# Value products of an attention stage: float32 matmuls on two halves of the array's columns in place of fp32r matmuls on high and low parts

## The chip, the cores and the metric

The kernel runs on one core of one Trainium2 chip. The metric is the device time of one execution in microseconds, the median of several runs. A profile, taken by the hardware profiler, shows one execution in detail. Engine names in it: PE is TensorE's matmuls and PEld its weight loads, DVE is VectorE, ACT is ScalarE, POOL is GpSimd, SP is SyncE, whose queue issues nearly all DMAs here.

## The reference

A trunk of two layers runs over 512 tokens and 16 learned meta tokens ahead of them (528 in all), 1024 wide, all in float32. In each layer one input projection gives the inputs of two mixers, a pooling mixer and a latent attention with 8 heads, and their gated sum goes through an output projection. Cut to what the change touches, the attention is:

```
kv = (c_kv @ w_kv_b).reshape(B, L, N_HEADS, QK_NOPE_DIM + V_HEAD_DIM)   # 64 + 64
k_nope, v = kv[..., :QK_NOPE_DIM], kv[..., QK_NOPE_DIM:]
...                                                                     # norms, rotary
s = einsum('bqhd,bkhd->bhqk', q, k) * scale      # causal, in blocks of 128 queries
p = softmax(where(valid, s, MASK_VALUE))
o = einsum('bhqk,bkhd->bqhd', p, v)
y_mla = (o.reshape(B, L, MLA_WIDTH) * silu(z_mla)) @ W_mla_up
```

Everything is float32, so the kernel has to keep float32's accuracy in its matmuls.

## The kernel before

**Numbers in two parts.** A matmul on fp32r operands keeps fewer bits than float32. The kernel therefore writes an operand as hi + lo, both fp32r: ScalarE copies the value into an fp32r tile (hi), VectorE subtracts hi from the value (lo). `mm3` (L204 to L208) makes a product from three matmuls, hi·hi, hi·lo and lo·hi. Nearly all of PE's work is of this kind: the rows of L205, L206 and L207. A few small sums (norms, L426, L501, L535, L707) are plain float32 matmuls with 16 or 32 columns of weights, placed with `tile_position=(0, 32 * g)` on four quarters of the array's columns.

**The main stream.** A generator, `stream`, walks a list of projections (`Gemm`s) in order. `step` issues its next few matmuls, `fill`, `fill_now` and `gap` issue as many as a given time would hold by a count in the code, and `after` hangs a step of the attention on that count. The projections so fill PE's time between the attention's matmuls. The framework's scheduler gives each engine its final order by readiness and the order of the code; `follow` ties two instructions of one engine in order without a wait, and `behind` makes an instruction wait for another, often the newest matmul of the stream.

**Attention, head by head.** `v_body` (L682) makes the values at the end of the projection v: for each of four blocks of 128 keys the result in PSUM is scaled and written to `vt`, 128 columns a head, 64 of hi (L700, ScalarE) and 64 of lo (L701, VectorE). `head` (L815) issues the scores of four blocks of 128 queries, their exponentials (`expo`) and 32x32 transposes on VectorE (`turn`) into the tile `attD`, which has ten blocks of 128 columns: the causal pairs of query block and key block. A DMA writes `attD` to DRAM (L906), and 7800 ns of the count later `back` (L912) issues four DMAs that read it back turned over into a tile `attE` (L915), keys on partitions. `parts` (L948) splits that tile, in two halves, into hi (L958, ScalarE, into a tile `th`) and lo (L959, VectorE, in place). `pv` (L962) makes the value products for the four key blocks j: key block j meets query blocks j to 3, so its matmul is 512, 384, 256 or 128 wide. For each j there are two matmuls into one PSUM tile `o`: at L980 all 128 columns of `vt` (hi and lo of the values) against hi of the probabilities, and at L983 the 64 columns of hi against lo. Rows 0 to 63 of `o` then hold hi·hi and hi·lo, rows 64 to 127 lo·hi. At L988 ScalarE copies one half of the rows, at L989 VectorE adds the other. The products of a head are issued while the scores of a later head are on their way: in `head`, `parts(prev)` comes first, then two gaps of main stream with the other work of the head, then `pv(late)`.

Of the kernel before, what the change touches and what calls it, by code (L numbers as in the profile page):

```python
# [9 lines left out]
F32 = mybir.dt.float32  # L10
F32R = mybir.dt.float32r
BF16 = mybir.dt.bfloat16
I32 = mybir.dt.int32
AF = mybir.ActivationFunctionType
ALU = mybir.AluOpType
# [3 lines left out]
P = 128  # L19
DEPTH = 2  # L20
D = 1024
# [3 lines left out]
HALF = T // 2  # L25
W = 528
WU = 544
H = 8
# [33 lines left out]
NB = 10  # L62
# [18 lines left out]
def trunk(ctx, tc, xT, xrow, mrow, pos, win, wkr, wqb, wkb, wvb, wgr, wpu, wmu, wout, gains, const, yT):  # L81
    nc = tc.nc
    pe, act, dve, gp, sp = nc.tensor, nc.scalar, nc.vector, nc.gpsimd, nc.sync

    cp = ctx.enter_context(tc.tile_pool(name="cp", bufs=1))
    sl = ctx.enter_context(tc.tile_pool(name="sl", bufs=1))
# [8 lines left out]
    def nm(s):  # L95
        uid[0] += 1
        return f"{s}_{uid[0]}"
# [5 lines left out]
        return tp.tile([P, w], F32, tag="tmp", name=nm("tmp"), bufs=3)  # L103

    def att(tag):
        return sl.tile([P, NB * P], F32 if tag == "D" else F32R, tag=f"att{tag}", name=nm(f"att{tag}"), bufs=1 if tag == "D" else 2)

    def wide():
        return tp.tile([P, NB * P], F32R, tag="th", name=nm("th"), bufs=2)

    def halves():
        for k in range(4, 8):
            for a, b in FULL:
                yield xb[:, k, a:b]
        for tag in "DE":
            t = att(tag)
            for a in range(4):
                yield t[:, HALF * a:HALF * a + HALF].bitcast(F32)

    def mmt():  # L120
        return pp.tile([P, 512], F32, tag="mm", name=nm("mm"), bufs=4)
# [56 lines left out]
    for j in range(2):  # L178
        gp.memset(qhl[0][j][96:128, :].bitcast(F32), 0.0)
        gp.memset(qhl[1][j][32:64, :].bitcast(F32), 0.0)  # L180
    vt = cp.tile([P, 4, H, P], F32R, name="vt")

    class Gemm:
        def __init__(self, name, src, width, evac=None, xs=None, segs=None, body=None):
# [25 lines left out]
    newest = [None]  # L210
# [95 lines left out]
    def follow(ins, other):  # L306
        tc.add_manual_dep(ins.ins, other.ins.name,
                          mybir.DependencyInfo(mybir.DependencyClass.NoSync, mybir.DependencyReason.SCHED_ONLY))

    def behind(ins, other):  # L310
        tc.add_manual_dep(ins.ins, other.ins.name,
                          mybir.DependencyInfo(mybir.DependencyClass.Sync, mybir.DependencyReason.DATA))
# [35 lines left out]
    class Layer:  # L348
# [333 lines left out]
        def v_body(self, k, w):  # L682
            self.vw.append(w)
            if k == 0:
                return
            wv, cs = self.vw, self.cs
            mc = sm.tile([P, 4 * NM], F32, tag="mc", name=nm("mc"))
            for k in range(2):
                h, l = (t[:, 0:NM].bitcast(F32).unsqueeze(1).to_broadcast([P, 2, NM]) for t in cs[k])
                dve.tensor_add(mc[:, 32 * k:32 * k + 32].rearrange("p (a b) -> p a b", a=2), h, l)  # L690
            self.vb = sm.tile([96, 512], F32R, tag="vb", name=nm("vb"))
            for j in range(4):
                ps = mmt()
                for k in range(2):
                    ch, cl = (t[:, NM + P * j:NM + P * (j + 1)] for t in cs[k])
                    mm3(ps, ch, cl, wv[k][0], wv[k][1], k == 0, k == 1)
                ci = self.ninv[:, j:j + 1]
                hi, lo = vt[:, j, :, 0:64], vt[:, j, :, 64:128]
                pv = ps.rearrange("p (a b) -> p a b", a=H)
                act.activation(hi, pv, AF.Copy, scale=ci)  # L700
                dve.scalar_tensor_tensor(out=lo, in0=pv, scalar=ci, in1=hi.bitcast(F32),  # L701
                                         op0=ALU.mult, op1=ALU.subtract)
                yield 6 * 216
            ps = mmt()
            for g in range(4):
                k, e = g % 2, 256 * (g // 2)
                mm = pe.matmul(ps[32 * g:32 * g + 32, 0:256], mc[:, 32 * k:32 * k + 32],  # L707
                               self.vgemm.raw[:, 512 * k + e:512 * k + e + 256], start=True, stop=True,
                               tile_position=(0, 32 * g))
                behind(mm, newest[0])  # L710
            vf, t = tmp(), tmp()
            for i in range(2):
                e = 256 * i
                act.activation(t[0:32, e:e + 256], ps[64 * i + 32:64 * i + 64, 0:256], AF.Copy)
                dve.tensor_add(t[0:32, e:e + 256], ps[64 * i:64 * i + 32, 0:256], t[0:32, e:e + 256])
            for e in range(2):
                v4 = [x[0:32, :512].rearrange("p (a e b) -> p a e b", a=4, e=2)[:, :, e, :] for x in (vf, t)]
                dve.tensor_scalar(v4[0], v4[1], self.ninv[0:32, 4:5], cst[0:32, C_VBD + e:C_VBD + e + 1],
                                  op0=ALU.mult, op1=ALU.mult)
            act.activation(self.vb[0:32, :], vf[0:32, :512], AF.Copy)  # L720
            dve.tensor_sub(self.vb[64:96, :], vf[0:32, :512], self.vb[0:32, :].bitcast(F32))
            act.activation(self.vb[32:64, :], vf[0:32, :512], AF.Copy)
            yield 6 * 216
# [91 lines left out]
        def head(self, h, kq, prev):  # L815
            kh, kl, qh, ql = kq
            odd = h % 2
# [85 lines left out]
            got = []  # L903
            n = NB * 32
# [7 lines left out]
            def back():  # L912
                got.append(att("E"))
                for b in range(4):
                    behind(sp.dma_start(got[0][32 * b:32 * b + 32, :].bitcast(F32).rearrange("k (a x) -> k a x", a=4),  # L915
                                        via[:, n * b:n * b + n].rearrange("(a k) x -> k a x", a=4)), newest[0])
                if odd == 0:
                    self.rb = slot("cq11")
                rb = self.rb
                behind(sp.dma_start(rb[64 * odd:64 * odd + 64, 0:512], row.partition_broadcast(64)), newest[0])  # L920
# [27 lines left out]
        def parts(self, prev):  # L948
            if prev is None:
                return None  # L950
            h, got = prev
            while not got:
                step()
            got = got[0]
            hi, f = wide(), got.bitcast(F32)
            for a in (0, NB * 64):
                b = a + NB * 64
                behind(act.activation(hi[:, a:b], f[:, a:b], AF.Copy), newest[0])  # L958
                dve.tensor_sub(got[:, a:b], f[:, a:b], hi[:, a:b].bitcast(F32))  # L959
            return h, hi, got  # L960

        def pv(self, prev, hosts=()):  # L962
            if prev is None:
                return
            h = prev[0]
            p, odd = h // 2, h % 2
            o = sct() if h == H - 1 else pp.tile([P, 512], F32, tag="o", name=nm("o"), bufs=1)
            hosts, last = list(hosts), [None]

            def chain(ins):  # L970
                if last[0] is not None:
                    follow(ins, last[0])
                last[0] = ins
                return ins

            for j in range(4):
                k0, n = block(j, j), 4 - j
                st = block(j + 1, j) - k0 if n > 1 else 1
                hi, lo = (t.rearrange("p (a s r) -> p s a r", a=4, s=NB)[:, k0:k0 + st * (n - 1) + 1:st] for t in prev[1:])
                chain(pe.matmul(o[:, P * j:512], vt[:, j, h, :], hi, start=j == 0, stop=j == 3))  # L980
                for fn in hosts[2 * j:2 * j + 2]:
                    chain(fn())
                chain(pe.matmul(o[0:64, P * j:512], vt[:, j, h, 0:64], lo, start=False, stop=j == 3, skip_group_check=True))  # L983
            if odd == 0:
                self.op = tmp()
            n0, m0 = (64, 0) if odd else (0, 64)
            op = self.op[n0:n0 + 64, NM:T]
            act.activation(op, o[m0:m0 + 64, :], AF.Copy)  # L988
            dve.tensor_add(op, o[n0:n0 + 64, :], op)  # L989
            if odd == 1:  # L990
                op, mt = self.op[:, NM:T], self.mt

                def part2():
                    m = mmt()
                    pe.matmul(m, self.vb[:, P * p:P * (p + 1)], mt[0:96, 0:512].rearrange("p (a i r) -> p i a r", a=4, i=4),  # L995
                              start=True, stop=True)
                    self.ogs[p] = (slot(f"q{p}", F32R), slot(f"kn{p}", F32R))
                    dve.tensor_add(op, m, op)
                    dve.tensor_mul(op, op, self.zms[p][:, NM:T])
                    split(*self.ogs[p], op, NM, T)  # L1000

                after((3 if p == 3 else 2) * LAG, part2)
# [293 lines left out]
```

## Time and profile before

| | |
|---|---|
| median of 3 runs | 756.11 us (755.23 to 756.22) |
| the profiled execution | 756.64 us, its span 754.9 us |
| PE busy | 749.7 us, 99% of the span |
| VectorE busy | 548.1 us |
| ScalarE busy | 395.9 us |
| HBM | 140 GB/s over the span |

The time of an execution is measured around the program; the span runs from its first to its last instruction in the profile. An instruction's duration on PE contains the depth of the pipeline, so matmuls that follow each other overlap in their rows, and what a matmul costs is read from its start to the start of the next. The attention of the first layer lies at about 163 to 312 us, that of the second at about 545 to 683 us. In rows such as `128*64 128x512` the first pair is rows and columns of the weights in the array, the second partitions and columns of the moving operand.

### The profile page before, as it was taken

To read this page: it belongs to the slowest core of one execution; us is meant where nothing else is said; L and a number is where in the kernel's file an instruction comes from. 1 tells how busy PE (TensorE), PEld (TensorE's weight loads), DVE (VectorE), ACT (ScalarE), POOL (GpSimd) and SP (SyncE) were. 2 spreads that over 40 slices of the span, in tenths; PEclk is the share of its full clock that TensorE was granted. 3 is DMA by queue.
4 is the path that set the end of the run, shared out by engine and by line. 5 is a ranking of instruction groups with operands and counts; after the bars stand their busy time and mean duration, and the time that the engine had idled before them with its cause. 6 is when DMAs were issued, how large, how long until landed. Compare 5 with 4: busy or idle time off the path is not lost.

```text
span 754.9 us, 14329 instructions
## 1 busy us (share of the span) xinstructions
PE 749.7 (99%) x5038; PEld 682.9 (90%) x5038; DVE 548.1 (73%) x1209; ACT 395.9 (52%) x866; POOL 218.8 (29%) x267
## 2 busy tenths in 40 slices
PE   9999999999999999999999999999999999999998
PEld 8999899999999999999997898887788888888887
DVE  5588777457999988684466477676478999975942
ACT  6755655645565665542355446456345666653321
POOL 1126404204463620061130264023044435111400
PEclk9999999999999999999999999999999999999999
DMA  8532223443765567525642322234447756773472
GB/s 316 162 108 89 74 82 86 113 116 119 211 186 166 151 194 192 156 86 157 183 145 85 114 84 66 89 90 120 108 135 210 190 156 181 195 200 93 127 227 84
DMA packets 72853, 106.58 MB, mean 141 GB/s; under 512 B 14102, under 2 KB 34966, under 8 KB 72780
## 3 DMA queue, kind: packets, MB, share of 16 engines
q1 hardware_dynamic: 72636, 105.39, 47.6%
q8 instruction: 40, 0.66, 0.4%
q14 instruction: 33, 0.27, 0.1%
q10 hardware_dynamic: 144, 0.26, 0.1%
HBM read 89.76 MB, written 15.86 MB: 140 GB/s over the span
## 4 chain that ended last, share of the span: by engine, by line
PE 98%; DMA 1%; ACT 0%; SPq 0%; issue 0%; DVE 0%; ACTq 0%
PE mm L205 29%; PE mm L207 29%; PE mm L206 29%; PE S L205 2%; PE S L207 2%; PE S L206 2%; PE o L980 1%; PE o L983 1%; PE S L535 1%; PE S L881 1%; DMA attE<-pdr 1%; PE S L501 0%; DMA xb<-xT 0%; PE mm L995 0%; PE mm L426 0%
## 5 line engine op out<-in xcount | busy, mean ns | idle before, releaser
L205 PE MATMUL mm<-hh,whi 128*128 128x264 f32 (+2 forms) x1072 | 336.1, 315 | 0.6 <-ACT whi L200 0.6
L206 PE MATMUL mm<-hl,whi 128*128 128x264 f32 (+2 forms) x1072 | 336.6, 315 | 0.0
L207 PE MATMUL mm<-hh,wlo 128*128 128x264 f32 (+2 forms) x1072 | 336.4, 316 | 0.0
L201 DVE TENSOR_TENSOR wlo<-raw,whi 128x512 fp32r<-128x512 f32 (+2 forms) x238 | 173.4, 730 | 95.8 <-ACT whi L200 92.4
L200 ACT ACTIVATE whi<-raw 128x512 fp32r<-128x512 f32 (+2 forms) x238 | 142.3, 600 | 176.1 <-PE mm L206 136.4
L205 PEld LDWEIGHTS mm<-hh,whi 128*128 128x128 f32 x1072 | 201.3, 188 | 15.0 <-issue 0.8
L206 PEld LDWEIGHTS mm<-hl,whi 128*128 128x128 f32 x1072 | 201.6, 188 | 12.9
L207 PEld LDWEIGHTS mm<-hh,wlo 128*128 128x128 f32 x1072 | 200.9, 188 | 12.3
L649 POOL TENSOR_TENSOR racc<-racc,tmp 128x264 f32<-128x264 f32 (+1 forms) x15 | 14.4, 959 | 132.3 <-ACT tmp L648 132.3
L1055 POOL TENSOR_TENSOR tmp<-tmp,xb 128x264 f32<-128x264 f32 (+1 forms) x24 | 27.0, 1137 | 49.1 <-DVE tmp L1053 46.4
L833 DVE CUSTOM_DVE_ANT_0 S<-S,maskw,nqs 128x240 f32<-128x240 f32 (+4 forms) x80 | 37.8, 492 | 4.2 <-PE S L207 3.9
L811 POOL CAST qhl<-q 32x528 fp32r<-32x528 f32 (+1 forms) x32 | 25.1, 800 | 44.2 <-PE S L881 42.9
L809 POOL CAST kh<-cq 32x528 fp32r<-32x528 f32 x16 | 15.6, 976 | 69.8 <-issue 36.1
L206 PE MATMUL mm<-th,whi 128*128 128x264 f32 (+1 forms) x108 | 34.7, 321 | 0.0
L205 PE MATMUL mm<-cq,whi 128*128 128x264 f32 (+1 forms) x108 | 34.7, 321 | 0.0
L205 PE MATMUL mm<-u,whi 128*128 128x264 f32 (+1 forms) x108 | 34.6, 321 | 0.0
L206 PE MATMUL mm<-cq,whi 128*128 128x264 f32 (+1 forms) x108 | 34.5, 321 | 0.0
L207 PE MATMUL mm<-cq,wlo 128*128 128x264 f32 (+1 forms) x108 | 34.5, 321 | 0.0
L207 PE MATMUL mm<-u,wlo 128*128 128x264 f32 (+1 forms) x108 | 34.5, 319 | 0.0
L959 DVE TENSOR_TENSOR attE<-attE,th 128x640 fp32r<-128x640 f32 x32 | 26.9, 862 | 3.7 <-ACT th L958 3.7
L840 ACT ACTIVATE cq<-S,bia 128x400 f32<-128x400 f32 (+2 forms) x48 | 24.4, 511 | 9.2 <-DVE bia L894 7.7
L843 POOL COPY pm<-cq 128x16 f32<-128x16 f32 x32 | 18.2, 570 | 37.7 <-ACT cq L840 37.5
(301 smaller groups left out, 1369.5 us busy)
## 6 DMA issues: line engine op xcount, KB each, us to landing
raw<-win SPq DMA_DIRECT2D x143, 256.0 KB, 3.2
pdr<-attD SPq DMA_DIRECT2D x16, 640.0 KB, 3.7
attE<-pdr SPq DMA_DIRECT2D x64, 160.0 KB, 3.9
raw<-wout SPq DMA_DIRECT2D x32, 256.0 KB, 2.8
raw<-wpu SPq DMA_DIRECT2D x16, 256.0 KB, 2.7
raw<-wmu SPq DMA_DIRECT2D x16, 256.0 KB, 2.7
raw<-wqb SPq DMA_DIRECT2D x12, 256.0 KB, 2.6
xb<-xT SPq DMA_DIRECT2D x8, 264.0 KB, 5.5
```

The lines of the kernel that those rows point to most:

```text
L200: act.activation(hi[:, :n], raw[:, :n], AF.Copy)
L201: dve.tensor_sub(lo[:, :n], raw[:, :n], hi[:, :n].bitcast(F32))
L205: first = pe.matmul(out, wh, xh, start=start, stop=False)
L206: pe.matmul(out, wh, xl, start=False, stop=False)
L207: newest[0] = pe.matmul(out, wl, xh, start=False, stop=stop)
L809: gp.tensor_copy(d[r0:r0 + 32, :], f[g0:g0 + 32, :])
L811: gp.tensor_copy(d[r0:r0 + 32, x0:T], f[g0:g0 + 32, x0:T])
L833: return dve.tensor_tensor_reduce(out=sv, in0=sv, in1=mask, scale=nqs[:, i, h:h + 1], scalar=3e38, op0=ALU.add, op1=ALU.min, accum_out=bia ...
L840: act.activation(pv, sv, AF.Exp, scale=-1.0, bias=bia[:, i:i + 1], accum_out=rs[:, c:c + 1])
L843: gp.tensor_copy(pm[:, i, 16 * odd:16 * odd + 16], pt[i][:, 0:NM])
L959: dve.tensor_sub(got[:, a:b], f[:, a:b], hi[:, a:b].bitcast(F32))
L1055: gp.tensor_add(t[:, :b - a], t[:, :b - a], self.am[m][:, a:b])
```

## The change

The probabilities and the values are no longer split. `vt` is a float32 tile with 64 columns a head, written by ScalarE alone. `attE` is float32, and `parts` only waits in the code until its loads have been issued. `pv` has one float32 matmul for each key block, with 64 columns of weights: blocks 0 and 3 go to one half of the array's columns and of `o`'s rows, blocks 1 and 2 to the other half, and each half sums its two blocks. ScalarE's copy and VectorE's add put the halves together; the first 128 queries meet key block 0 alone, so the add leaves them out.

```
 def att(tag):
-    return sl.tile([P, NB * P], F32 if tag == "D" else F32R, ...)
+    return sl.tile([P, NB * P], F32, ...)
...
-vt = cp.tile([P, 4, H, P], F32R, name="vt")
+vt = cp.tile([P, 4, H, 64], F32, name="vt")
...                                                # v_body
-    hi, lo = vt[:, j, :, 0:64], vt[:, j, :, 64:128]
-    pv = ps.rearrange("p (a b) -> p a b", a=H)
-    act.activation(hi, pv, AF.Copy, scale=ci)
-    dve.scalar_tensor_tensor(out=lo, in0=pv, scalar=ci, in1=hi.bitcast(F32),
-                             op0=ALU.mult, op1=ALU.subtract)
+    act.activation(vt[:, j], ps.rearrange("p (a b) -> p a b", a=H), AF.Copy, scale=ci)
...                                                # parts
-    got = got[0]
-    hi, f = wide(), got.bitcast(F32)
-    for a in (0, NB * 64):
-        b = a + NB * 64
-        behind(act.activation(hi[:, a:b], f[:, a:b], AF.Copy), newest[0])
-        dve.tensor_sub(got[:, a:b], f[:, a:b], hi[:, a:b].bitcast(F32))
-    return h, hi, got
+    return h, got[0]
...                                                # pv
-    for j in range(4):
+    n0, m0 = (64, 0) if odd else (0, 64)
+    for j in (0, 1, 2, 3):
         k0, n = block(j, j), 4 - j
         st = block(j + 1, j) - k0 if n > 1 else 1
-        hi, lo = (t.rearrange("p (a s r) -> p s a r", a=4, s=NB)[...] for t in prev[1:])
-        chain(pe.matmul(o[:, P * j:512], vt[:, j, h, :], hi, start=j == 0, stop=j == 3))
-        for fn in hosts[2 * j:2 * j + 2]:
-            chain(fn())
-        chain(pe.matmul(o[0:64, P * j:512], vt[:, j, h, 0:64], lo, start=False, stop=j == 3, ...))
+        x = prev[1].rearrange("p (a s r) -> p s a r", a=4, s=NB)[...]
+        c = m0 if j in (0, 3) else n0
+        mm = pe.matmul(o[c:c + 64, P * j:512], vt[:, j, h, :], x, start=j < 2, stop=j > 1, tile_position=(0, c))
+        if j:
+            follow(mm, last)
+        last = mm
...
     act.activation(op, o[m0:m0 + 64, :], AF.Copy)
-    dve.tensor_add(op, o[n0:n0 + 64, :], op)
+    dve.tensor_add(op[:, P:512], o[n0:n0 + 64, P:512], op[:, P:512])
```

More of the change, by code (lines that the diff above doesn't have):

```diff
@@ L105, in att @@
     def att(tag):
-        return sl.tile([P, NB * P], F32 if tag == "D" else F32R, tag=f"att{tag}", name=nm(f"att{tag}"), bufs=1 if tag == "D" else 2)
+        return sl.tile([P, NB * P], F32, tag=f"att{tag}", name=nm(f"att{tag}"), bufs=1 if tag == "D" else 2)
     def wide():
@@ L117, in halves @@
             for a in range(4):
-                yield t[:, HALF * a:HALF * a + HALF].bitcast(F32)
+                yield t[:, HALF * a:HALF * a + HALF]
     def mmt():
@@ L914, in back @@
                 for b in range(4):
-                    behind(sp.dma_start(got[0][32 * b:32 * b + 32, :].bitcast(F32).rearrange("k (a x) -> k a x", a=4),
+                    behind(sp.dma_start(got[0][32 * b:32 * b + 32, :].rearrange("k (a x) -> k a x", a=4),
                                         via[:, n * b:n * b + n].rearrange("(a k) x -> k a x", a=4)), newest[0])
@@ L953, in parts, with pv @@
                 step()
-            got = got[0]
-            hi, f = wide(), got.bitcast(F32)
-            for a in (0, NB * 64):
-                b = a + NB * 64
-                behind(act.activation(hi[:, a:b], f[:, a:b], AF.Copy), newest[0])
-                dve.tensor_sub(got[:, a:b], f[:, a:b], hi[:, a:b].bitcast(F32))
-            return h, hi, got
-        def pv(self, prev, hosts=()):
+            return h, got[0]
+        def pv(self, prev):
             if prev is None:
@@ L967, in pv @@
             o = sct() if h == H - 1 else pp.tile([P, 512], F32, tag="o", name=nm("o"), bufs=1)
[L968 to L974, printed above, removed]
-            for j in range(4):
+            n0, m0 = (64, 0) if odd else (0, 64)
+            for j in (0, 1, 2, 3):
                 k0, n = block(j, j), 4 - j
                 st = block(j + 1, j) - k0 if n > 1 else 1
-                hi, lo = (t.rearrange("p (a s r) -> p s a r", a=4, s=NB)[:, k0:k0 + st * (n - 1) + 1:st] for t in prev[1:])
-                chain(pe.matmul(o[:, P * j:512], vt[:, j, h, :], hi, start=j == 0, stop=j == 3))
-                for fn in hosts[2 * j:2 * j + 2]:
-                    chain(fn())
-                chain(pe.matmul(o[0:64, P * j:512], vt[:, j, h, 0:64], lo, start=False, stop=j == 3, skip_group_check=True))
+                x = prev[1].rearrange("p (a s r) -> p s a r", a=4, s=NB)[:, k0:k0 + st * (n - 1) + 1:st]
+                c = m0 if j in (0, 3) else n0
[3 more added lines that the diff above has]
+                last = mm
             if odd == 0:
                 self.op = tmp()
-            n0, m0 = (64, 0) if odd else (0, 64)
             op = self.op[n0:n0 + 64, NM:T]
             act.activation(op, o[m0:m0 + 64, :], AF.Copy)
-            dve.tensor_add(op, o[n0:n0 + 64, :], op)
+            dve.tensor_add(op[:, P:512], o[n0:n0 + 64, P:512], op[:, P:512])
             if odd == 1:
```

## The prediction

> **What bounds the kernel now.** First the first parts of the profile's page: the span, the busy times, the granted clock, the chain that ended last.
>
> ```profile
> span 754.9 us, 14329 instructions
> PE 749.7 (99%) x5038; PEld 682.9 (90%) x5038; DVE 548.1 (73%) x1209; ACT 395.9 (52%) x866; POOL 218.8 (29%) x267
> PEclk9999999999999999999999999999999999999999
> PE 98%; DMA 1%; ACT 0%; SPq 0%; issue 0%; DVE 0%; ACTq 0%
> ```
>
> The clock is full in all 40 slices, and 98% of the chain is PE. The change works in the two attention stages, so I cut the span there (busy time by stretch):
>
> ```profile
> 163.00:312.00 149.00, 148.95 (x1206) 147.42 (x1205) 126.47 (x331) 87.18 (x216) 53.77 (x72) 1.00 0.62 176
> 545.00:683.00 138.00, 138.00 (x670) 115.39 (x669) 119.92 (x275) 80.39 (x185) 48.50 (x72) 1.00 0.65 181
> ```
>
> The first column after the length is PE: 148.95 of 149.00 us and 138.00 of 138.00. The projections of the main stream fill every hole there, so PE never runs dry. VectorE is at 126.47 of 149.00 and 119.92 of 138.00, high but off the path. Only PE time counts: the question is how many us of array time the value products take before and after.
>
> **The value products now.** Sixteen heads with eight matmuls each, in these groups (by line: least, median and greatest duration, first and last start):
>
> ```profile
> L980 PE MATMUL o<-th,vt x56: 223/310/502, 210.1 to 673.1; 128*128 128x512 f32 x14, 128*128 128x384 f32 x14, 128*128 128x256 f32 x14, 128*128 128x128 f32 x14
> L980 PE MATMUL S<-th,vt x8: 223/313/403, 305.9 to 679.7; 128*128 128x512 f32 x2, 128*128 128x384 f32 x2, 128*128 128x256 f32 x2, 128*128 128x128 f32 x2
> L983 PE MATMUL o<-attE,vt x56: 220/312/404, 212.4 to 673.2; 128*64 128x512 f32 x14, 128*64 128x384 f32 x14, 128*64 128x256 f32 x14, 128*64 128x128 f32 x14
> L983 PE MATMUL S<-attE,vt x8: 221/311/403, 307.3 to 679.8; 128*64 128x512 f32 x2, 128*64 128x384 f32 x2, 128*64 128x256 f32 x2, 128*64 128x128 f32 x2
> ```
>
> Durations contain the pipeline's depth, so I count from start to start. A head whose eight stand together, and one that comes behind small matmuls (PE in order of time):
>
> ```profile
> 671.85 0.40 PE L206 MATMUL mm<-hl,whi 128*128 128x512 f32 x1
> 672.08 0.40 PE L980 MATMUL o<-th,vt 128*128 128x512 f32 x1
> 672.32 0.40 PE L983 MATMUL o<-attE,vt 128*64 128x512 f32 x1
> ...
> 673.20 0.23 PE L983 MATMUL o<-attE,vt 128*64 128x128 f32 x1
> 673.27 0.44 PE L207 MATMUL mm<-hh,wlo 128*128 128x512 f32 x1
> 673.55 0.39 PE L205 MATMUL mm<-hh,whi 128*128 128x512 f32 x1
> ```
>
> ```profile
> 221.53 0.17 PE L881 MATMUL S<-kh,qhl 128*16 128x16 f32 x1
> 221.56 0.48 PE L980 MATMUL o<-th,vt 128*128 128x512 f32 x1
> ...
> 222.84 0.33 PE L205 MATMUL mm<-hh,whi 128*128 128x264 f32 x1
> 223.02 0.28 PE L206 MATMUL mm<-hl,whi 128*128 128x264 f32 x1
> ```
>
> An ordinary 128x512 step is 0.23 to 0.24 us (671.85 to 672.08, 672.08 to 672.32), or 0.46 ns a column, and here the half-wide pass over low parts costs as much as the full one. The first head: 672.08 to 673.27 is 1.19, and the next step (673.27 to 673.55) is 0.28, 0.05 over its like: 1.24 us. The second: 221.56 to 222.84 is 1.28, plus 0.18 less 0.12 (a 128x264 step, below) behind it: 1.34. The same sum over the 128 rows of the four groups gives 1.23 to 1.56 us a head, 20.7 us together, 1.29 in the mean.
>
> **What takes their place.** Per head four float32 matmuls with 64 columns of weights: blocks 0 (512 wide) and 3 (128) on one half of the array's columns, blocks 1 (384) and 2 (256) on the other. No float32 matmul 64 columns wide is in the trace, but there are float32 matmuls on quarters of the columns, at L426, L501, L535 and L707. They give both prices. The pass:
>
> ```profile
> 405.21 0.41 PE L426 MATMUL mm<-cq,ones 128*32 128x264 f32 x1
> 405.22 0.41 PE L426 MATMUL mm<-q,ones 128*32 128x264 f32 x1
> 405.22 0.41 PE L426 MATMUL mm<-cq,ones 128*32 128x264 f32 x1
> 405.23 0.41 PE L426 MATMUL mm<-q,ones 128*32 128x264 f32 x1
> 405.46 0.39 PE L426 MATMUL mm<-cq,ones 128*32 128x264 f32 x1
> ...
> 406.12 1.96 PE L501 MATMUL S<-xb,kn 128*32 128x264 f32 x32
> 408.02 0.50 PE L205 MATMUL mm<-hh,whi 128*128 128x512 f32 x1
> 408.36 0.40 PE L206 MATMUL mm<-hl,whi 128*128 128x512 f32 x1
> ```
>
> L501 is written 16 times a layer and stands here x32: a float32 matmul is two passes. Four passes start within 0.02 us on the four quarters, the next four follow when these are through. The 32 are eight rounds of four: 1.96 less the last one's own 0.39 is 1.57 us for seven rounds, 0.224 us for 264 columns, or 0.85 ns a column, 1.85 times the 0.46 above. So a float32 matmul costs two passes of nearly double price each, but quarters run side by side at no visible loss. If halves do the same, block 0 and block 3 take 640 x 2 x 0.85 = 1.09 us, blocks 1 and 2 the same 640 columns, 1.09, beside it. The order 0, 1, 2, 3 fits: when block 0 ends (0.87), block 2's second pass starts and block 3 takes its half.
>
> That alone would be 0.2 us less than 1.29. But entering and leaving such a burst costs:
>
> ```profile
> 85.70 0.40 PE L207 MATMUL mm<-whi,kl 128*128 128x512 f32 x1
> 86.03 0.64 PE L707 MATMUL mm<-attD,mc 128*32 128x256 f32 x8
> 86.59 0.39 PE L205 MATMUL mm<-hh,whi 128*128 128x264 f32 x1
> 86.82 0.28 PE L206 MATMUL mm<-hl,whi 128*128 128x264 f32 x1
> 86.94 0.28 PE L207 MATMUL mm<-hh,wlo 128*128 128x264 f32 x1
> ```
>
> From 85.70 to 86.82 is 1.12 us. The two ordinary steps in it are 0.23 (512 wide) and 0.12 (264 wide, 86.82 to 86.94), which leaves 0.77 for the burst. Its eight passes are two rounds of 256 columns, 2 x 256 x 0.85 = 0.44. So 0.33 us are fixed: about 0.10 ahead, where the array's last full matmul must be through before the first weights go in, 0.23 behind, where the first full weights wait in the same way. The burst of the fence before leaves as slowly: its last passes are through at about 407.92 (406.12 + 1.57 + 0.224), and the second ordinary matmul comes at 408.36 instead of 408.15 (407.92 + 0.23), 0.21 later. The next rows add a little, since the first weights of a half take longer to load than those of a quarter:
>
> ```profile
> L983 PEld LDWEIGHTS o<-attE,vt x56: 133/135/139, 212.3 to 673.1; 128*64 128x64 f32 x56
> L707 PEld LDWEIGHTS mm<-attD,mc x16: 106/108/110, 86.0 to 465.5; 128*32 128x32 f32 x16
> ```
>
> That is 0.03 us once a burst. A head then takes 1.09 + 0.33 + 0.03 = 1.45 us, against 1.29: 0.16 x 16 = 2.5 us more.
>
> The Trainium skill, "TensorEngine Tiling (Array Packing)", section Key Properties, says that a change of tiling mode, not just of the tile, drains the array; it gives no price. The trace agrees, with the 0.33 us above. The page "TensorE: Matmul & The Clock Gate" of the Trainium skill, Part 3, speaks against the overlap itself: matmuls start and end strictly in program order. Here four starts stand within 0.02 us ahead of any fifth, and if the two passes of a matmul lie side by side in the queue, as one instruction's parts would, the second pass of the first was overtaken by the first passes of the other quarters. No row shows the queue's order, so this becomes a rival below.
>
> **What else goes or moves.**
>
> ```profile
> L958 ACT ACTIVATE th<-attE x32: 721/724/741, 206.4 to 674.9; 128x640 fp32r<-128x640 f32 x32
> L959 DVE TENSOR_TENSOR attE<-attE,th x32: 761/810/2182, 207.5 to 675.8; 128x640 fp32r<-128x640 f32 x32
> ```
>
> Off ScalarE go 32 copies, 32 x 0.72 = 23 us; off VectorE 32 subtracts, 32 x 0.81 = 26 us by the median, and the subtracts of L701, and a quarter of each add at L989. Worth to the end: nothing, because PE in these stages idles 0.05 us in 287. It could cost only if the freed engines let something else collide; every load keeps its issue (SP's queue is unchanged, 64 loads of attE), so I see nothing. The value tile shrinks by half, which nobody waits for.
>
> A wait moves: the products now wait on the four loads of attE themselves, on PE, where the copy on ScalarE stood between. Behind a waiting product stands the whole main stream. The chain of waits passes through the loads of attE at one head alone, the seventh of the first layer (start, length; below it PE in order of time):
>
> ```profile
> 285.25 4.36 DMA attE<-pdr
> ...
> 291.13 0.50 PE o L980
> ```
>
> ```profile
> 290.80 0.28 PE L205 MATMUL mm<-hh,whi 128*128 128x264 f32 x1
> ```
>
> The load lands at 289.61, the copies follow, and PE starts at 291.13, 0.33 behind a matmul whose step is 0.12: it stands idle for 0.2 us. Without the copies the product can come up to 1.5 us earlier; the cost of that wait lies between 0 (a load that is in when PE comes) and 1.5 us (a product queued just as early as the copies' absence allows, and a load that is late by as much). I take 0.2, as now, nearest to the row, so the difference is nil. In the other direction the readiness of all four products at one moment is a help: today the first head's low parts start at 212.4 and its high parts at 210.1 (first starts of the two groups), with projections between; from now on nothing should split the four.
>
> **Sum.** 16 x (1.45 - 1.29) = +2.5 us. The profiled run of before took 756.64 us with a span of 754.9; the median is 756.11, so the profiled one lies 0.5 above it. The forecast for the median is 756.1 + 2.5 = 758.6 (0.33%). What a measurement of this kernel can tell from no change is about 0.2%, 1.5 us.
>
> **The rivals.**
>
> *Passes start strictly in order.* Block 1's first pass then cannot start before block 0's second, at 0.435: block 1 ends at 1.09, block 2 at 1.52, and block 3 inside that. 1.52 + 0.36 = 1.88 a head, +0.59 x 16 = +9.4: 765.5 us. Against it: the four starts within 0.02 us. For it: they are on quarters, and the queue's order isn't shown. Chance 0.07.
>
> *Halves do not overlap at all.* 2 x 1.09 + 0.36 = 2.54 a head, +1.25 x 16 = +20: 776 us. Only if two 64-wide halves share something that four quarters do not; no row hints at it. 0.04.
>
> *The four are split by main-stream matmuls*, as the pairs are today. Block 0 alone (0.87), then the rest (1.09), and 0.36 twice: 2.68, +1.39 a head; in half of the heads +11: 767 us. Against it: all four wait for the same loads. 0.05.
>
> *Faster: the switch is free.* The point that decides is whether the 0.33 us belong to the change of the array's split or to something else that those bursts have (other buffers, waits of their own). With 0.03 instead of 0.36 a head takes 1.12, 16 x -0.17 = -2.7 us: 753.4. Part 3 of the Trainium skill's page "TensorE: Matmul & The Clock Gate" counts a packed group as one matmul's duration and about 4 ns for each further tile, with no charge for the switch. Against it: the two bursts shown, of different lines and lengths, leave equally slowly, 0.21 and 0.23. 0.08.
>
> *In between: a cheaper switch*, 0.13 to 0.29 us with the weights' 0.03 in it, as when the half-wide weights go in earlier: 1.22 to 1.38 a head, -1.1 to +1.4 us, no measurable change. 0.14.
>
> **How the numbers follow.** The forecast has 0.62: with the wait's 1.5 us above it and 0.06 us a head (1 us) below, its own range is 757.6 to 760.1. Adding the cheaper switch gives 755.5 at the low end. Leaving the free switch (0.08), the serial halves (0.04) and half of the split heads (0.03) outside, the range goes to 766, past the strict order: 755.5 to 766 holds 0.85. Slower by over 0.2%: 0.62 + 0.07 + 0.04 + 0.05 = 0.78; within: 0.14; faster: 0.08.
>
> **What would show it.** In the profile after: four value matmuls a head as eight rows of 64 columns, the first rows of block 0 and of block 1 within some 0.02 us of each other; from the last ordinary matmul ahead to the second behind, less their two steps, 1.45 us; PE still busy for all of both stages. Wrong would be a first pass of block 1 that starts 0.4 us or more behind block 0's (strict order or no overlap), a projection between the four, a PE wait on attE's loads of over a microsecond, or a burst that takes under 1.3 us.

## The result, and the profile after

The changed kernel takes 761.89 us (761.51 to 762.47), the one before 756.16 (755.23 to 757.16) beside it: a ratio of 1.0070 (95% interval 1.0060 to 1.0081), 5.7 us slower. The forecast was 2.5 us slower, 758.6. The page of the profile after, and busy time by stretch (length, PE, PE weights, VectorE, ScalarE, GpSimd, clock, DMA share, GB/s):

```profile
span 759.7 us, 14198 instructions
PE 754.8 (99%) x5038; PEld 676.7 (89%) x5038; DVE 521.2 (69%) x1169; ACT 376.6 (50%) x834; POOL 206.2 (27%) x267
PE 99%; DMA 0%; issue 0%; ACT 0%; DVE 0%; SPq 0%; DVEq 0%; ACTq 0%
```

```profile
163.00:312.00 149.00, 149.00 (x1195) 143.45 (x1194) 117.74 (x316) 76.72 (x201) 44.18 (x72) 1.00 0.62 175
545.00:683.00 138.00, 138.00 (x653) 108.56 (x652) 106.99 (x257) 70.28 (x168) 45.65 (x72) 1.00 0.63 178
```

PE is busy through both attention stages as before, and every other engine has less to do. The number of PE's instructions is the same, 5038: two passes of a float32 matmul have taken the place of the two fp32r matmuls of each key block. What PE waited for, in the whole span:

```profile
PE wps L157 <- DVE na L760: 1.1, 1, 1.1
PE mm L205 <- DVE u L584: 0.7, 1, 0.7
```

No wait on a load of attE is among them, and over the span PE is idle no longer than before (759.7 less 754.8 is 4.9 us, before it was 5.2). So PE has more work, and only the products were changed on it. A whole head (PE in order of time; below it the products between 221.70 and 221.76 us: least, median and greatest duration, first and last start):

```profile
221.61 0.17 PE L877 MATMUL S<-kl,qhl 128*16 128x16 f32 x1
221.64 0.17 PE L877 MATMUL S<-kh,qhl 128*16 128x16 f32 x1
221.74 1.30 PE L964 MATMUL o<-attE,vt 128*64 128x512 f32 x8
222.97 0.39 PE L205 MATMUL mm<-hh,whi 128*128 128x264 f32 x1
223.19 0.29 PE L206 MATMUL mm<-hl,whi 128*128 128x264 f32 x1
```

```profile
L964 PE MATMUL o<-attE,vt x2: 537/590/643, 221.7 to 221.7; 128*64 128x512 f32 x1, 128*64 128x384 f32 x1
```

Two passes start within 0.01 us: the first of block 0 and the first of block 1, on the two halves. From 221.64 to 223.19 is 1.55 us; less the steps of the two matmuls around it (0.02 and 0.12) the head costs 1.41, where the prediction had 1.45. But this is not what every head looks like:

```profile
608.94 0.40 PE L207 MATMUL mm<-hh,wlo 128*128 128x512 f32 x1
609.27 1.07 PE L964 MATMUL o<-attE,vt 128*64 128x512 f32 x4
610.27 0.50 PE L205 MATMUL mm<-hh,whi 128*128 128x512 f32 x1
610.60 0.40 PE L206 MATMUL mm<-hl,whi 128*128 128x512 f32 x1
610.93 0.65 PE L964 MATMUL o<-attE,vt 128*64 128x256 f32 x2
611.50 0.50 PE L207 MATMUL mm<-hh,wlo 128*128 128x512 f32 x1
611.84 0.39 PE L205 MATMUL mm<-hh,whi 128*128 128x512 f32 x1
...
615.64 0.30 PE L205 MATMUL S<-kh,qhl 96*128 96x288 f32 x1
615.87 0.43 PE L964 MATMUL o<-attE,vt 128*64 128x128 f32 x2
616.23 0.50 PE L205 MATMUL mm<-hh,whi 128*128 128x512 f32 x1
616.57 0.39 PE L206 MATMUL mm<-hl,whi 128*128 128x512 f32 x1
```

Here other matmuls stand between the products: blocks 0 and 1, then block 2, then block 3, in three bursts (stretches in which the array is split). By the same sum they cost 1.20 (608.94 to 610.60), 0.78 (610.60 to 611.84) and 0.57 us (615.64 to 616.57), 2.55 together. The two passes of block 2 (256 columns) are 0.43 us at 0.84 ns a column, and the burst costs 0.35 more; those of block 3 (128 columns) are 0.21, and the burst costs 0.36 more. So each part of a torn head pays the price of a burst again, and blocks 2 and 3 run beside nothing. Over all rows of L964, twelve heads stand whole at 1.41 to 1.47 us, and four are torn, at 1.96, 2.00, 2.55 and 2.61 (the first of both layers, the third and the fifth of the second). All 16 come to 26.3 us against 20.7 before: 5.6 more, about as much as the medians differ. The spans of the two profiled executions differ by 4.8 us; the profiled one of before lies 0.5 us above its median.

### The profile page after: what moved, and what is told of

The parts are those of the page before. It is cut to its first block, busy times and chain, and to the rows that moved or that the text cites. A ratio compares the mean times of both kernels' runs of the same rounds, so it can differ in the third digit from the quotient of the medians.

```text
span 759.7 us, 14198 instructions
## 1 busy us (share of the span) xinstructions
PE 754.8 (99%) x5038; PEld 676.7 (89%) x5038; DVE 521.2 (69%) x1169; ACT 376.6 (50%) x834; POOL 206.2 (27%) x267
## 4 chain that ended last, share of the span: by engine, by line
PE 99%; DMA 0%; issue 0%; ACT 0%; DVE 0%; SPq 0%; DVEq 0%; ACTq 0%
PE mm L205 29%; PE mm L207 29%; PE mm L206 29%; PE o L964 3%; PE S L205 2%; PE S L206 2%; PE S L207 2%; PE S L535 1%; PE S L877 1%; PE S L501 0%; DMA xb<-xT 0%; PE S L964 0%; PE mm L978 0%; PE mm L426 0%; PE mm L703 0%
## 5 line engine op out<-in xcount | busy, mean ns | idle before, releaser
L201 DVE TENSOR_TENSOR wlo<-raw,whi 128x512 fp32r<-128x512 f32 (+2 forms) x238 | 175.2, 738 | 111.4 <-ACT whi L200 104.3
L839 POOL COPY pm<-cq 128x16 f32<-128x16 f32 x32 | 12.2, 380 | 66.8 <-ACT cq L836 66.3
L842 DVE STREAM_TRANSPOSE attD<-cq 128x256 f32<-128x256 f32 (+2 forms) x48 | 21.1, 464 | 2.2 <-ACT cq L836 2.2
```

Of the source, the lines that this page charges most:

```text
L201: dve.tensor_sub(lo[:, :n], raw[:, :n], hi[:, :n].bitcast(F32))
L842: ins = dve.transpose(grid[:, :, k:k + n, :].rearrange("p b s r -> p s b r"), pt[i][:, NM + P * j:NM + P * (j + n)])
```

## The experiments

### The four products kept together

```
-    mm = pe.matmul(o[c:c + 64, P * j:512], vt[:, j, h, :], x, ...)
+    with tc.high_priority() if j else ExitStack():
+        mm = pe.matmul(o[c:c + 64, P * j:512], vt[:, j, h, :], x, ...)
```

> The changed kernel with one thing more: the scheduler must put a head's four products next to each other (the last three get a high priority once the first is placed). Theory (A): what the change costs over the prediction is that the scheduler tore four of the 16 heads apart, and each further burst pays the change of the array's split again; the twelve whole heads cost 1.41 to 1.47 us of array time each. Then 16 x 1.43 = 22.9 us against 20.7 of before: 756.2 + 2.2 = 758.4 us, and all 16 heads in one burst of 1.41 to 1.47. Rival (B): the torn heads cost nothing, since the main stream fills the holes, and the excess is lost elsewhere: 761.9 us as now.

Measured: 759.02 us, a ratio of 1.0037 (1.0024 to 1.0051), span 757.3 against 759.7 of the changed kernel. The head that was in three bursts (PE in order of time):

```profile
608.66 0.40 PE L207 MATMUL mm<-hh,wlo 128*128 128x512 f32 x1
608.99 1.30 PE L965 MATMUL o<-attE,vt 128*64 128x512 f32 x8
610.22 0.50 PE L205 MATMUL mm<-hh,whi 128*128 128x512 f32 x1
610.56 0.40 PE L206 MATMUL mm<-hl,whi 128*128 128x512 f32 x1
```

608.66 to 610.56 less two steps of 0.23 is 1.44 us, in place of 2.55. All 16 heads now cost 1.41 to 1.47, 22.9 together, 2.2 more than before; the span is 2.4 longer. (A) holds and (B) falls: tearing the heads cost 2.4 us by the spans, 2.5 by the medians (each against the kernel before beside it) and 3.4 by the rows. What stays is the price that the prediction worked out.

### One half, and the full array

```
# one half, on the kernel with the products together
-    mm = pe.matmul(o[c:c + 64, P * j:512], ..., start=j < 2, stop=j > 1, tile_position=(0, c))
+    mm = pe.matmul(o[n0:n0 + 64, P * j:512], ..., start=j == 0, stop=j == 3, tile_position=(0, n0))
...
# full array, on the kernel with the products together
-vt = cp.tile([P, 4, H, 64], F32, name="vt")
+vt = cp.tile([P, 4, H, P], F32, name="vt")
+gp.memset(vt[:, :, :, 64:128], 0.0)
...
+    mm = pe.matmul(o[:, P * j:512], vt[:, j, h, :], x, start=j == 0, stop=j == 3)
...
```

> As e1_together, but all four products of a head go to the same half of the array's columns, which then sums all four blocks (no add of two halves is needed). Theory (A), the two halves of the change run side by side and a burst has a fixed price of about 0.36 us: the passes now follow each other, 1280 columns x 2 x 0.83 ns = 2.13 us, 2.5 us a head, 16 x 2.5 - 20.7 = +19: 775 us. Rival (C), the halves hardly overlap in the changed kernel and the fixed price is smaller than thought: little more than e1_together, 758 to 762 us.

> As e2_one_half, float32 products one after the other, but without a split of the array: 128 columns of weights, 64 of values beside 64 of zeros, no tile position. It tells whether the fixed price belongs to the change of the array's split or to float32. Theory (A), the split: no fixed price, 2.13 + 0.06 = 2.2 us a head, 16 x 2.2 - 20.7 = +14.5: 770.7 us. Rival (D), a change between fp32r and float32 costs it, split or not: 2.5 us a head, 775 us as e2_one_half.

Measured: 775.69 us (1.0263, 1.0244 to 1.0281) on one half, 770.79 us (1.0198, 1.0179 to 1.0216) on the full array. The same head in both, first on one half, then on the full array:

```profile
254.87 0.17 PE L877 MATMUL S<-kh,qhl 128*16 128x16 f32 x1
254.97 2.37 PE L964 MATMUL o<-attE,vt 128*64 128x512 f32 x8
257.27 0.39 PE L205 MATMUL mm<-hh,whi 128*128 128x264 f32 x1
257.50 0.28 PE L206 MATMUL mm<-hl,whi 128*128 128x264 f32 x1
```

```profile
253.77 0.17 PE L878 MATMUL S<-kh,qhl 128*16 128x16 f32 x1
253.79 2.40 PE L965 MATMUL o<-attE,vt 128*128 128x512 f32 x8
255.95 0.37 PE L206 MATMUL mm<-hh,whi 128*128 128x264 f32 x1
256.16 0.28 PE L207 MATMUL mm<-hl,whi 128*128 128x264 f32 x1
```

On one half the head takes 254.87 to 257.50, less 0.02 and 0.12: 2.49 us, and over 16 heads 2.50 in the mean. On the full array it takes 2.25 (253.77 to 256.16), 2.21 in the mean. Two readings follow. The two halves of the changed kernel do run side by side: taking that away costs 1.07 us a head (2.50 less 1.43), which is the array time of one half, so (C) falls. And the fixed price belongs to the split: with the same float32 passes on an unsplit array it is 0.3 us a head less, so (D) falls. Nor is it the narrower weights alone: before the change the products of L983 had 64 columns of weights on the unsplit array, and a 512 wide step of theirs was 0.24 us, as with 128 columns. In the rows it lies on both sides: 0.10 against 0.02 us ahead of the first pass (start to start, 254.87 to 254.97 and 253.77 to 253.79), the rest between the first pass and the second ordinary matmul.

### One burst for two heads

```
-    for j in (0, 1, 2, 3):                    # one head: blocks 0, 3 and 1, 2 on the two halves
-        mm = pe.matmul(o[c:c + 64, ...], vt[:, j, h, :], x, start=j < 2, stop=j > 1, tile_position=(0, c))
+    for j in range(4):                        # two heads: one on each half
+        for h, got in kept[i:i + 2][::-1]:
+            c = 64 * (h % 2)
+            mm = pe.matmul(o[c:c + 64, ...], vt[:, j, h, :], x, start=j == 0, stop=j == 3, tile_position=(0, c))
...
-    act.activation(op, o[m0:m0 + 64, :], AF.Copy)
-    dve.tensor_add(op[:, P:512], o[n0:n0 + 64, P:512], op[:, P:512])
+    act.activation(self.op[:, NM:T], o, AF.Copy)
```

> Products wait until an odd head's probabilities are there too, and both heads' eight products go in one burst: the even head on one half of the array's columns, the odd head on the other, each summing its four blocks there (so one copy takes out both, and no add is needed; three tiles attE instead of two). Theory (A), the fixed price is one of the burst: 8 bursts x (2.13 + 0.36) = 19.9 us, 0.8 less than before: 755.4 us. Rival (E), it is one of each head's four matmuls: 16 x 1.43 = 22.9, 758.4 us as e1_together. Rival (F), the products come later and something behind them waits: over 759 us, with idle PE.

Measured: 755.83 us, a ratio of 0.9999 (0.9990 to 1.0008), span 753.7. PE in order of time:

```profile
249.89 0.17 PE L878 MATMUL S<-kh,qhl 128*16 128x16 f32 x1
249.99 2.38 PE L970 MATMUL o<-attE,vt 128*64 128x512 f32 x16
252.29 0.39 PE L205 MATMUL mm<-hh,whi 128*128 128x264 f32 x1
252.52 0.28 PE L206 MATMUL mm<-hl,whi 128*128 128x264 f32 x1
```

Two heads take 2.49 us (249.89 to 252.52, less 0.02 and 0.12), what one takes on one half. Eight bursts come to 20.2 us, 0.5 less than before; the span is 1.2 shorter, and the time can't be told from that of before. (E) falls: eight products in a burst pay the same price as four. (F) falls as well: no wait of PE on these products is in the profile.

### The split work put back

```
...                                          # parts, of the kernel with the products together
-    return h, got[0]
+    hi, f = wide(), got[0]
+    for a in (0, NB * 64):
+        b = a + NB * 64
+        behind(act.activation(hi[:, a:b], f[:, a:b], AF.Copy), newest[0])
+        dve.tensor_sub(hi[:, a:b], f[:, a:b], hi[:, a:b].bitcast(F32))
+    return h, f
```

> e1_together with the 32 copies on ScalarE and the 32 subtracts on VectorE put back, into a tile that nobody reads. Theory (A), the freed engines gave the end nothing, since PE alone sets it: as e1_together, 759.0 us within 1. Rival (G), e1_together already holds a gain from the freed engines that hides part of the products' price: slower by more than 1.5 us, with idle PE in the attention stages.

Measured: 759.15 us, 1.0041 (1.0028 to 1.0055), span 757.2. Busy time by stretch:

```profile
163.00:312.00 149.00, 149.00 (x1197) 143.91 (x1197) 127.03 (x331) 85.84 (x214) 47.44 (x72) 1.00 0.61 173
545.00:683.00 138.00, 137.48 (x661) 110.38 (x660) 118.67 (x276) 81.46 (x185) 48.08 (x72) 1.00 0.65 178
```

VectorE is back at 127.03 and 118.67 us, as before the change, and the time is that of the kernel without this work (759.02). In the second stage PE is idle for 0.52 us, ahead of the last head's products (PE in order of time; in brackets the idle time and what ended it):

```profile
674.81 1.30 PE L970 MATMUL S<-attE,vt 128*64 128x512 f32 x8 [0.52 <-DMA attE<-pdr]
```

(G) falls even so: some 48 us of work put back on ScalarE and VectorE cost nothing that can be measured, so freeing these engines gave nothing either.

### Another order of the four

```
-    for j in (0, 1, 2, 3):
+    for j in (0, 3, 1, 2):
```

> e1_together with the four products in the order 0, 3, 1, 2: both products of one half are queued ahead of both of the other. Theory (A), passes of the two halves overtake each other freely in PE's queue: the first passes of blocks 0 and 1 still start within 0.02 us, 1.43 us a head, 759.0 us. Rival (H), a pass can overtake only a little (one matmul that waits): block 1 starts when block 3's first pass comes up or later, 0.43 to 0.85 us behind block 0, so 1.85 to 2.3 us a head, 766 to 773 us. If passes started strictly in the order of the code, it would be 1.07 + 1.07 + 0.36 = 2.5 us a head, 776 us.

Measured: 758.33 us, 1.0030 (1.0018 to 1.0042), span 756.2. The value products between 220.70 and 220.82 us:

```profile
L965 PE MATMUL o<-attE,vt x2: 537/590/643, 220.8 to 220.8; 128*64 128x512 f32 x1, 128*64 128x384 f32 x1
```

Block 1's first pass (128x384) still starts with block 0's (128x512), though the whole of block 3's matmul is ahead of it in the code. A head costs 1.42 to 1.48 us. (H) falls. The span is 1.1 us shorter than with the order 0, 1, 2, 3, while the heads cost 0.1 more in all; the intervals of the two times overlap, and what made that difference is open.

### One burst for four heads

```
-    if len(self.kept) < 2:
+    if len(self.kept) < 4:
```

and four tiles attE in place of three.

> As e5_pairs with four heads in one burst: the products wait until every fourth head's probabilities are there, and sixteen go in one burst, two pairs after each other (four tiles attE, the second pair's sum in another PSUM tile). Theory (A), the fixed price is one of the burst: 4 x (4 x 1.07 + 0.36) = 18.6 us against 20.7 of before: 755.8 - 2.1 = 753.7 us, and 1.4 less than e5_pairs. Rival (F), the late products hold up what comes behind them (the tiles attE, the gated outputs, the last projection): no gain over e5_pairs, or slower, with idle PE or with the loads of attE late.

> e8_quads, in which the first pair of every four was given the meta tokens' probabilities of the second pair; here each pair has a tile of its own for them (a slot that is free by then), and nothing is left out. Theory (A), with 4 bursts of 4 x 1.07 + 0.36 = 4.64 us, 18.6 us in all: as e8_quads, 754.7 us, faster than before by 0.1 to 0.3%. Rival (F): the second tile's loads or its slot hold something up and the time is 755.9 or more.

In the first of the two, the first pair of every four is given the meta tokens' probabilities of the second pair, and its own are left out. The change from the first to the second (cut):

```
-    self.mt = slot("racc", F32R)
+    self.mts[p] = slot("kp" if p % 2 else "racc", F32R)
...
```

Measured: 754.73 us for the first, 0.9982 (0.9973 to 0.9991), and 754.84 us for the second, 0.9986 (0.9977 to 0.9995), span 752.8. The second, PE in order of time:

```profile
247.37 0.17 PE L878 MATMUL S<-kh,qhl 128*16 128x16 f32 x1
247.47 2.37 PE L970 MATMUL S<-attE,vt 128*64 128x512 f32 x16
249.67 2.32 PE L970 MATMUL o<-attE,vt 128*64 128x512 f32 x16
251.93 0.39 PE L205 MATMUL mm<-hh,whi 128*128 128x264 f32 x1
252.15 0.28 PE L206 MATMUL mm<-hl,whi 128*128 128x264 f32 x1
```

The two pairs follow each other with no gap, and four heads take 4.64 us (247.37 to 252.15, less 0.02 and 0.12). Four bursts come to 18.6 us, 2.1 less than before, and the span is 2.1 shorter (752.8 against 754.9). The second, which leaves nothing out, is faster than the kernel before and the changed one, by 0.14% (0.05 to 0.23%) against the one before. That is about 1.1 us by the times, half of what the rows give.

One, two and four heads in a burst cost 1.43, 2.52 and 4.65 us in the mean over all bursts. From two to four heads that is 1.07 us for each head, and what is left is 0.36, 0.38 and 0.38 us: the price of a burst. Two lengths fix such a line, so the third, one head, is the test of it: it is off by 0.02 us.

## Why the prediction was right or wrong

**PE alone sets the time: right.** PE is at 149.00 of 149.00 and 138.00 of 138.00 us after, and the split work put back left the time as it was.

**A head's products before, 1.29 us: right within 0.06 us.** With it the rows of every kernel give the difference to the kernel before to within 1 us over 16 heads, from the one half (+19.4 us by the rows, +19.9 by the medians) to four heads in a burst (-2.1 and -1.3).

**The pass, 0.85 ns a column, two of them, halves side by side: right.** A head's array time is 1.07 us by the series of bursts, against 1.09, and on one half the same passes cost twice that. The rivals of the strict order and of no overlap are out; the strict order was tested with a harder order than the change has.

**The fixed price, 0.33 + 0.03 us: right**, 0.36 to 0.38 by the three lengths. That it belongs to the split is shown by the full array, where 0.3 us of it go. So the rival of a free switch is out. The Trainium skill, "TensorEngine Tiling (Array Packing)", section Key Properties, says that changing the tiling mode drains the array. The runs agree in that the change costs these 0.3 us; none shows whether by a drain.

**The moved wait and the freed engines, nothing: right.** In the changed kernel PE waits on no load of attE, and the kernel with the split work put back is at 759.15 us against 759.02.

**The step that failed: "from now on nothing should split the four".** It was argued from readiness: all four wait for the same loads. That removes one reason for a split (the late low parts), not the scheduler's freedom to put another matmul between. In the trace every wait on a semaphore stands at or ahead of a torn head's first product; those of its later bursts wait for nothing, so the order put them there, not a late operand. Four of 16 heads were torn, at 9.1 us in place of 5.7, and these 3.4 us are as large as the gap between forecast and result, 3.3. The prediction had this as a rival with a chance of 0.05 and a price for half of the heads; a quarter of the heads was torn. The result, 761.9, lies above the forecast's own range of 757.6 to 760.1. The wide range holds it because it was drawn up to 766, past the strict order, with half the chance of split heads inside: most of that room was left for a cause that the runs ruled out, and in so far it is luck that the range holds.

Before the change a tear cost nothing: in 14 of the 16 heads the first product stood apart from the other seven, and such a head cost 1.23 to 1.27 us, or 1.33 to 1.34 behind small matmuls, as whole heads did (1.24 and 1.34; one more, at 1.56, contains PE's wait at 291.13). One such product before the change, with an ordinary step of 0.23 us (PE in order of time):

```profile
591.24 0.39 PE L206 MATMUL mm<-hl,whi 128*128 128x512 f32 x1
591.48 0.40 PE L980 MATMUL o<-th,vt 128*128 128x512 f32 x1
591.71 0.39 PE L207 MATMUL mm<-hh,wlo 128*128 128x512 f32 x1
```

After the change every tear costs a burst's price and, where it parts blocks that would lie side by side, their overlap. Why the scheduler chose these four was not tried: what is shown is that putting them together takes the loss away.

The sign was right, and without tears the sum was too: the kernel with the products together is at +2.2 us by the rows and +3.2 by the medians (interval 1.8 to 3.9), where the forecast had +2.5.

## What to carry to other kernels

On a kernel that PE bounds, count the stretches in which the array is split, and not only the columns. Here each cost 0.36 to 0.38 us, as much as some 800 columns of an fp32r matmul at 0.46 ns, so a saving by packing has to be larger than that for each burst, and work of the same split belongs in one burst. When a change makes neighbours matter, make them neighbours. The order among the four was given in the changed kernel and did not keep others out; raising the priority of the last three did. Splitting into high and low parts on engines that were not the bound cost nothing here, and taking that work away gained nothing.

## What the runs showed of the hardware that was not expected

The passes of the two halves overtake each other further than had to be supposed. With the whole matmul of block 3 ahead of it in the code, block 1's first pass on the other half still started with block 0's first. "TensorE: Matmul & The Clock Gate" of the Trainium skill, Part 3, has matmuls start and end strictly in program order; here the rows of the order 0, 3, 1, 2 do not agree with that for the starts, at 0.01 us between block 0's and block 1's first pass. At the end of the same head, block 2's second pass, the last in the code, starts 0.09 us ahead of block 3's second.
